# Seven-product output projection: blocks of positions change places, T2 and T3 are made within the attention, T1 and B11 are split where they are made

## The chip, the core and the metric

The kernel runs on one core of one Trainium2 chip. The engines named are PE (TensorE: matmuls and transposes), DVE (VectorE), ACT (ScalarE), POOL (GpSimd) and SP (SyncE), whose queue issues the transfers here. PEld is the weight load of PE. The metric is the device time of one execution in microseconds; before the change the median of three runs is 2041.89 us (2041.83 to 2044.91).

## What is computed

One layer of a hybrid decoder, in float32, on 2048 positions of width 1024:

```python
h = rmsnorm(x, norm1_g[l])
proj = h @ w_in[l]
p_q, p_k, p_v, p_g, p_a, c_b, c_c, c_h = jnp.split(proj, splits, axis=-1)
...
gate_logits = (p_a @ w_gate_up[l] + b_gate[l]).astype(jnp.float32)
log_a = (jax.nn.log_sigmoid(gate_logits) / GATE_NORMALIZER).reshape(bsz, seq, GLA_HEADS, GLA_DK)
o = gla_chunked(q, k, v, log_a)
o = rmsnorm(o, gla_norm_g[l]).astype(x.dtype)
o = o * jax.nn.silu(p_g.reshape(bsz, seq, GLA_HEADS, GLA_DV))
o_gla = o.reshape(bsz, seq, GLA_WIDTH)
u = c_c * c_h
o_conv = c_b * causal_depthwise_conv(u, conv_w[l])
mixed = jnp.concatenate([o_gla, o_conv], axis=-1) @ w_out[l]
x = x + mixed
h2 = rmsnorm(x, norm2_g[l])
ffn = (jax.nn.silu(h2 @ w_ffn_gate[l]) * (h2 @ w_ffn_up[l])) @ w_ffn_down[l]
x = x + ffn
```

A last RMSNorm follows. `gla_chunked` is causal gated linear attention with 4 heads (keys of 64, values of 128); the forget gate is low-rank. The short convolution has width 3 over 512 channels.

## The kernel before

**Products.** Each float32 operand is split into an upper part `hi` (rounded to a reduced float32 form, by ACT, L206) and a lower part `lo` (the rest, by DVE, L207). A product takes three matmuls, hi by hi, hi by lo and lo by hi (L503 to L505). A *unit* (`unit`) makes a 2 by 2 block product in seven block products instead of eight, in the manner of Strassen and Winograd: from the blocks B11, B12, B21, B22 of the moving side it needs T1 = B12 - B11, T2 = B22 - T1, T3 = B22 - B12 and T4 = T2 - B21 (up to sign), and from the weights S1 to S4. In each product four slices of 128 (`k`) are summed. Results go from PSUM by ACT as copies `c` (L549) or are added by DVE (L537).

**Positions and stages.** The 2048 positions form four blocks of 512; half 0 is blocks 0 and 1, half 1 is blocks 2 and 3. In time: the opening, the input projection of half 0 (to 269 us), that of half 1 (`in_proj(1)`, twelve units, 269 to 565), the output projection of half 0 by seven products (`out_proj_in_sevens`, four units, 565 to 666), that of half 1 by plain products (`out_proj`, from 666), then the FFN. For the seven products of the output projection the rows are the attention's output (`s_gla`) and the convolution's (`s_mix`), the columns blocks 0 and 1: B11 and B12 are the convolution's output of blocks 0 and 1, B21 and B22 the attention's.

**Order of the work.** PE runs the products. Beside them a list `background` holds generators (stepwise programs); `tick` is called after each block product and advances the first of them by one step at every second product, at every product while `hurry` is set, at three of four while `hasty` is set. At `in_proj(1)` the list holds a pause, `gate(1)` (the forget gate of half 1, hurried), `gla_half(0)` (the attention of half 0, eight chunks of 128 positions, hasty for its first 20 steps) and `mix_differences` (T3, T2 and T4, in four steps of 128 channels, hurried), then `gla_half(1)`, which runs on into the seven products. T1 is made and stored in `in_proj(0)`, in the conv units. `drain_background` runs what is left before the next stage starts. The scheduler places the instructions of a step on each engine's queue, and the engines work their queues in order. All transfers go through SP's queue, in order, a transfer waiting for one eight places back in a rotation.

**Operands.** The buffer `op` (28 of them, tag `op`) holds one block slice as a pair hi, lo. `load_pair` loads a stored pair; `load_undivided` loads a whole block, split later: at the end of the unit's second, fourth, fifth and sixth product for those named in `due`. In `mix_operands`, B11 and T1 are loaded whole and split before the first product; T2 is loaded as a pair; the rest are split by `due`. For half 1, `build_mix` loads pairs: the conv blocks of half 1 are split in `in_proj(1)` and stored as pairs, as are the attention's. `behind(marks)` orders an instruction behind given earlier ones, such as the last copy (`last_out`) or addition (`last_plus`).

## Time and profile before

| quantity | value |
|---|---|
| median of three runs | 2041.89 us |
| profiled execution | 2044.2 us |
| its span | 2042.4 us |
| PE busy | 2010.8 us, 98% |
| DVE busy | 77% |
| ACT busy | 48% |
| granted TensorE clock, mean | 0.993 |
| DMA, mean | 209 GB/s |

The page gives the span of one profiled execution, 1.8 us shorter than the execution's time. A row of the timeline reads: start, length, engine, line, operation, tile written <- tiles read, shape, count, and in brackets the idle time of that engine before it with what ended it. A row of the waits reads: engine, tile and line that waited <- what ended the wait, then us in total, times, longest. The shares of PE's chain go to the three product lines, 27 to 28% each.

### The profile page before, as it was taken

How to read it: one execution, taken by the hardware profiler on the slowest of the kernel's cores; microseconds unless marked ns; L12 is line 12 of the kernel's file. 1: busy time of each engine (PE TensorE's matmuls, PEld its weight loads, DVE VectorE, ACT ScalarE, POOL GpSimd, SP SyncE). 2: the span in 40 equal slices, each digit the busy share in tenths (PEclk: the TensorE clock that was granted, in tenths of full speed). 3: DMA queues.
4: the chain of work that ended last, by engine and by line, in shares of the span. 5: the costliest groups of instructions: out<-in, count | busy, mean ns of one | idle time of the engine just before them, and what ended most of it. 6: DMA issues, size and time to landing. Idle time of an engine off the chain costs nothing.

```text
span 2042.4 us, 27016 instructions
## 1 busy us (share of the span) xinstructions
PE 2010.8 (98%) x9251; PEld 1652.8 (81%) x9251; DVE 1574.5 (77%) x2831; ACT 981.9 (48%) x1941; POOL 10.3 (1%) x17
## 2 busy tenths in 40 slices
PE   9999999998989999999999999999999999999998
PEld 8888877787868888888888888887888888888886
DVE  7878868558887787778777688887777767778886
ACT  6664455654654344444444452334434444454345
POOL 0000000000000000000000000000000000000001
PEclk9999999999989999999999999999999999999998
DMA  7356865437687973446445576577444444486653
GB/s 263 128 202 219 285 260 176 135 122 266 194 277 246 346 269 134 170 171 219 164 159 196 192 292 242 188 283 292 157 168 170 158 147 170 175 331 221 247 216 129
DMA packets 192426, 427.78 MB, mean 209 GB/s; under 512 B 20544, under 2 KB 63776, under 8 KB 182816
## 3 DMA queue, kind: packets, MB, share of 16 engines
q1 hardware_dynamic: 191568, 425.40, 58.5%
q8 instruction: 73, 1.20, 0.2%
q10 hardware_dynamic: 720, 0.66, 0.1%
q14 instruction: 65, 0.53, 0.1%
HBM read 280.22 MB, written 145.75 MB: 209 GB/s over the span
## 4 chain that ended last, share of the span: by engine, by line
PE 94%; DVE 2%; ACT 2%; DMA 1%; issue 0%; SPq 0%; POOL 0%; POOLq 0%; DVEq 0%; ACTq 0%
PE mm L503 28%; PE mm L505 27%; PE mm L504 27%; PE mm L1394 1%; PE mm L1391 1%; PE mm L1392 1%; PE a_ps L1030 1%; PE mm L811 1%; PE mm L813 1%; PE mm L812 1%; PE o_ps L1211 1%; PE mm L1711 1%; DMA op<-sdT 1%; DVE wq L207 0%; PE o_ps L1218 0%
## 5 line engine op out<-in xcount | busy, mean ns | idle before, releaser
L503 PE MATMUL mm<-op,wq 128*128 128x512 f32 x2555 | 997.7, 393 | 9.2 <-ACT c L549 6.5
L504 PE MATMUL mm<-op,wq 128*128 128x512 f32 x2555 | 995.3, 390 | 0.0
L505 PE MATMUL mm<-op,wq 128*128 128x512 f32 x2555 | 985.9, 391 | 3.2 <-DVE wq L207 3.0
L206 ACT ACTIVATE wq<-raw 128x512 fp32r<-128x512 f32 (+2 forms) x620 | 362.1, 588 | 594.7 <-PE mm L505 500.3
L503 PEld LDWEIGHTS mm<-op,wq 128*128 128x128 f32 x2555 | 480.8, 188 | 115.9 <-ACT c L549 8.1
L505 PEld LDWEIGHTS mm<-op,wq 128*128 128x128 f32 x2555 | 480.7, 188 | 105.8 <-DVE wq L207 5.2
L504 PEld LDWEIGHTS mm<-op,wq 128*128 128x128 f32 x2555 | 481.1, 188 | 99.6 <-DVE op L207 1.5
L207 DVE TENSOR_TENSOR wq<-raw,wq 128x512 fp32r<-128x512 f32 (+2 forms) x620 | 390.9, 635 | 148.5 <-ACT wq L206 146.7
L537 DVE TENSOR_TENSOR y<-mm,y 128x512 f32<-128x512 f32 x213 | 145.6, 687 | 68.8 <-PE mm L505 67.9
L537 DVE TENSOR_TENSOR c<-mm,c 128x512 f32<-128x512 f32 x196 | 134.6, 687 | 74.3 <-PE mm L505 69.4
L549 ACT ACTIVATE c<-mm 128x512 f32<-128x512 f32 x198 | 115.3, 588 | 31.6 <-PE mm L505 28.4
L455 DVE TENSOR_TENSOR raw<-raw 128x512 f32<-128x512 f32 (+2 forms) x190 | 118.7, 631 | 2.2
L206 ACT ACTIVATE wq<-s 128x512 fp32r<-128x512 f32 (+2 forms) x100 | 58.9, 589 | 111.9 <-PE mm L505 98.5
L455 DVE TENSOR_TENSOR s<-raw 128x512 f32<-128x512 f32 (+2 forms) x95 | 60.0, 631 | 29.0 <-DMA raw<-in_wffn_dram 17.2
L207 DVE TENSOR_TENSOR op<-op 128x512 fp32r<-128x512 f32 x118 | 77.5, 682 | 3.7 <-ACT op L206 3.6
L206 ACT ACTIVATE op<-op 128x512 fp32r<-128x512 f32 x118 | 68.2, 621 | 11.4 <-DMA op<-sgla 5.2
L207 DVE TENSOR_TENSOR wq<-s,wq 128x512 fp32r<-128x512 f32 (+2 forms) x100 | 63.4, 634 | 2.1 <-ACT wq L206 1.3
L455 DVE TENSOR_TENSOR raw<-s,raw 128x512 f32<-128x512 f32 (+2 forms) x95 | 60.1, 633 | 1.4
L607 ACT ACTIVATE sg<-mm 128x512 f32<-128x512 f32 x26 | 15.5, 598 | 87.4 <-PE mm L505 87.3
L607 ACT ACTIVATE c<-c 128x512 f32<-128x512 f32 x78 | 48.9, 629 | 13.1 <-DVE c L537 10.5
L1392 PE MATMUL mm<-op,wq 128*128 128x512 f32 x128 | 50.2, 392 | 0.0
L1391 PE MATMUL mm<-op,wq 128*128 128x512 f32 x128 | 49.8, 389 | 0.0
(234 smaller groups left out, 1546.3 us busy)
## 6 DMA issues: line engine op xcount, KB each, us to landing
raw<-in_wffn_dram SPq DMA_DIRECT2D x44, 1024.0 KB, 6.2
sa_B<-so SPq DMA_DIRECT2D x47, 512.0 KB, 3.6
op<-sa_B SPq DMA_DIRECT2D x47, 512.0 KB, 6.5
raw<-in_win_dram SPq DMA_DIRECT2D x22, 1024.0 KB, 5.7
sa_T<-so SPq DMA_DIRECT2D x44, 512.0 KB, 4.4
op<-sa_T SPq DMA_DIRECT2D x44, 512.0 KB, 6.9
raw<-in_wdown_dram SPq DMA_DIRECT2D x24, 768.0 KB, 5.5
sx<-y SPq DMA_DIRECT2D x48, 256.0 KB, 4.1
```

Source lines behind the costliest of these rows:

```text
L206: last_hi[:] = [act.activation(hi, src, AF.Copy)]
L207: last_lo[:] = [dve.tensor_tensor(lo, src, hi.bitcast(F32), ALU.subtract)]
L455: dve.tensor_tensor(*args)
L503: pe.matmul(o[:], wh, xh, start=first and k == 0, stop=False, skip_group_check=True)
L504: pe.matmul(o[:], wh, xl, start=False, stop=False, skip_group_check=True)
L505: return pe.matmul(o[:], wl, xh, start=False, stop=k == n - 1, skip_group_check=True)
L537: last_plus[:] = [dve.tensor_tensor(t[:], o[:], t[:], ALU.add)]
L549: last_out[:] = [act.activation(t[:], o[:], AF.Copy)]
L607: last_silu[:] = [act.activation(s[:], c[:], AF.Silu)]
L811: pe.matmul(acc[:], wq[:, 0, c], p[:, 0, :], start=first, stop=False)
L1391: pe.matmul(o[e, j][:], wh, m[:, 0, :], start=n == 0, stop=False)
L1392: pe.matmul(o[e, j][:], wh, m[:, 1, :], start=False, stop=False)
```

## The change

The blocks change places: block 1's conv output becomes B11, block 0's B12, block 1's attention B21 and block 0's B22 (the residual `xt[1 - j]` and `s_x1[1 - j]` follow). T1 is then conv 0 - conv 1, T2 = attention 0 - T1 and T3 = attention 0 - conv 0, none of which needs block 1's attention; only T4 = T2 - attention 1 does.

- `gate(1)` is no longer hurried; it and what follows it run at three of four products (`hastened(..., 70)`).
- `mixes_early` makes T3 and T2 in four steps between the steps of the attention, once block 0's attention is done; T2 is split and stored as a pair and whole (`s_whole`). `mixes_late` makes T4 from the whole T2 after the attention. They use four small tiles (`mixed_tile`) instead of the tag of `h`.
- T1 and B11 are split in `in_proj(0)`, where they are made, and stored as pairs (`s_pair`), so `mix_operands` loads three operands as pairs.
- The conv blocks of half 1 are stored whole and split in `build_mix` (`load_whole`).
- In `in_proj(1)` the first two units, not three, have their weights prepared in step (`after=2`); `gla_half(1)` has one step more at its start.

```diff
@@ -113,11 +113,12 @@
-    s_mix = [
-        [dram.tile([P] + parts[b] + [PB], F32, name=f"sm{b}_{k}") for k in range(4)]
-        for b in range(NB)
-    ]
+    s_mix = scratch("sm", 4)
+    s_pair = {
+        n: [dram.tile([P, 2, PB], F32, name=f"sp{n}_{k}") for k in range(4)] for n in ("B11", "T1")
+    }
     s_gla = [dram.tile([P, HEADS] + parts[b] + [PB], F32, name=f"sgla{b}") for b in range(NB)]
+    s_whole = [dram.tile([P, PB], F32, name=f"sw{k}") for k in range(4)]
@@ -318,6 +319,7 @@
             if i == n:
                 hasty.clear()
             yield
+        hasty.clear()
 
     def h1_paced():
         with_marks.append(True)
@@ -1083,7 +1085,7 @@
             if half == 0:
                 yield unit(win[2], ops, raw=raw, between=between, rest=rest)
             for u in range(0 if half else 3, 12):
-                yield unit(win[u], ops, after=2 if half and u < 3 else None)
+                yield unit(win[u], ops, after=2 if half and u < 2 else None)
 
         units = units()
         for dst, i0 in ((s_kq, 0), (s_kq, 2), (s_v, 0), (s_v, 2)):
@@ -1119,19 +1121,20 @@
             for r, j, c, _ in next(units):
                 y = made[r, j] = cc[r, j]
                 dve.tensor_tensor(y[:], c[:], y[:], ALU.mult)
-                if half == 0:
-                    store(s_mix[j][i0 + r][:], y[:])
-                    if (r, 1 - j) in made:
-                        t1 = tt("t1")
-                        dve.tensor_tensor(t1[:], made[r, 1][:], made[r, 0][:], ALU.subtract)
-                        store(s_diff["T1"][i0 + r][:], t1[:])
-                    continue
-                hi = tp.tile([P, PB], F32R, name="hi", tag="t")
-                split(y[:], hi[:], y[:].bitcast(F32R))
-                dst = s_mix[2 * half + j][i0 + r]
-                store(dst[:, 0, :], hi[:].bitcast(F32))
-                store(dst[:, 1, :], y[:])
-
+                if half == 0 and (r, 1 - j) in made:
+                    t1 = tt("t1")
+                    dve.tensor_tensor(t1[:], made[r, 0][:], made[r, 1][:], ALU.subtract)
+                    store(s_diff["T1"][i0 + r][:], t1[:])
+                    store_pair(s_pair["T1"][i0 + r], t1)
+                    store_pair(s_pair["B11"][i0 + r], made[r, 1])
+                if half or j == 0:
+                    store(s_mix[2 * half + j][i0 + r][:], y[:])
+
+    def store_pair(dst, y):
+        hi = tp.tile([P, PB], F32R, name="hi", tag="t")
+        split(y[:], hi[:], y[:].bitcast(F32R))
+        for e, p in enumerate((hi[:].bitcast(F32), y[:])):
+            store(dst[:, e, :], p)
 
     def gla_half(half):
         chunks = [(b, t) for b in (2 * half, 2 * half + 1) for t in range(PT)]
@@ -1139,6 +1142,8 @@
             tables = act.preload_act_table_set("natural_log_exp_and_others")
         fetched = gla_fetch(*chunks[0])
         yield
+        if half:
+            yield
         with tc.issue_after(tables.ins):
             cur = gla_scaled(*fetched)
         yield
@@ -1150,6 +1155,7 @@
                 fetched = gla_fetch(*chunks[n + 1])
             if o is not None:
                 yield from gla_finish(*chunks[n - 1], *o)
+                done.add(chunks[n - 1])
             o = gla_outputs(b, t, *s)
             if n + 1 < len(chunks):
                 cur = gla_scaled(*fetched)
@@ -1287,57 +1293,66 @@
             act.activation(q[:], y, AF.Square)
             dve.tensor_tensor(ssq[:], ssq[:], q[:], ALU.add)
 
-    def mix_differences():
-        hurry.append(True)
-
-        def fetch(k):
-            tiles = []
-            for src in (s_mix[1][k][:], s_gla[1][:, k], s_diff["T1"][k][:], s_gla[0][:, k]):
-                tiles.append(bt("h"))
-                load(tiles[-1][:], src)
-            return tiles
-
-        def subtract(y, a, b):
-            with behind(last_plus):
-                dve.tensor_tensor(y[:], a[:], b[:], ALU.subtract)
-
-        tiles = fetch(0)
-        yield
+    def mixes_within(attention):
+
+        made = mixes_early()
+        for _ in attention:
+            yield
+            if (0, PT - 1) in done and next(made, True) is None:
+                yield
+        yield from made
+        yield from mixes_late()
+        done.add("mixes")
+
+    def mixed_tile(name, i):
+        tag = ("ssx0", "ssx1", "rb", "rb")[i]
+        return tiny.tile([P, PB], F32, name=name, tag=tag, bufs=1 if i < 2 else 2)
+
+    def mix_tiles(srcs, first=0):
+        tiles = [mixed_tile("mx", first + i) for i in range(len(srcs))]
+        for y, src in zip(tiles, srcs):
+            load(y[:], src)
+        return tiles
+
+    def subtract(y, a, b):
+        with behind(last_plus):
+            dve.tensor_tensor(y[:], a[:], b[:], ALU.subtract)
+
+    def mixes_early():
+
         for k in range(4):
-            b12, b22, t1, b21 = tiles
+            t1, b22, b12 = mix_tiles((s_diff["T1"][k][:], s_gla[0][:, k], s_mix[0][k][:]))
+            yield
             subtract(b12, b22, b12)
             store(s_diff["T3"][k][:], b12[:])
             subtract(b22, b22, t1)
-            if k < 3:
-                tiles = fetch(k + 1)
-            yield
-            subtract(b21, b21, b22)
-            store(s_diff["T4"][k][:], b21[:])
-            hi = bx[0].tile([P, PB], F32R, name="hi", tag="b")
+            store(s_whole[k][:], b22[:])
+            hi, lo = mixed_tile("hi", 3), t1
             with behind(last_out + last_plus):
-                split(b22[:], hi[:], b22[:].bitcast(F32R))
-            for e, p in enumerate((hi, b22)):
-                store(s_diff["T2"][k][:, e, :], p[:].bitcast(F32))
-            yield
-        hurry.clear()
-        done.add("mixes")
-
-    def hurried(steps):
-        hurry.append(True)
-        yield from steps
-        hurry.clear()
+                split(b22[:], hi[:].bitcast(F32R), lo[:].bitcast(F32R))
+            for e, y in enumerate((hi, lo)):
+                store(s_diff["T2"][k][:, e, :], y[:])
+            yield
+
+    def mixes_late():
+        for k in (0, 2):
+            pairs = [
+                mix_tiles((s_whole[k + i][:], s_gla[1][:, k + i]), 2 * i) for i in range(2)
+            ]
+            yield
+            for i, (t2, b21) in enumerate(pairs):
+                subtract(t2, b21, t2)
+                store(s_diff["T4"][k + i][:], t2[:])
+            yield
 
     def mix_operands():
-        src = {"B11": [y[:] for y in s_mix[0]], "B21": [s_gla[0][:, k] for k in range(4)]}
-        src.update({"B22": [s_gla[1][:, k] for k in range(4)], **s_diff})
+        src = {"B21": [s_gla[1][:, k] for k in range(4)]}
+        src.update({"B22": [s_gla[0][:, k] for k in range(4)], **s_diff, **s_pair})
         ops = no_operands()
         for _, n in PRODUCTS:
-            ops[n] = [(load_pair if n == "T2" else load_undivided)(p) for p in src[n]]
-            if n in ("B11", "T1"):
-                with behind(last_out):
-                    for o in ops[n]:
-                        split(o[:, 1, :].bitcast(F32), o[:, 0, :], o[:, 1, :])
-            elif n != "T2":
+            paired = n in ("B11", "T1", "T2")
+            ops[n] = [(load_pair if paired else load_undivided)(p) for p in src[n]]
+            if not paired:
                 undivided[n] = ops[n]
         return ops
 
@@ -1348,7 +1363,7 @@
                 y[r, j] = tt("y")
             else:
                 y[r, j] = tiny.tile([P, PB], F32, name="y", tag="rb")
-            load(y[r, j][:], xt[j, :, d0 + r, :])
+            load(y[r, j][:], xt[1 - j, :, d0 + r, :])
         return y
 
     def out_proj_in_sevens(first, ops):
@@ -1368,13 +1383,16 @@
             unit(None, ops, onto=onto[d0], raw=quads, midway=more)
             for r, j in ((0, 0), (1, 1), (0, 1), (1, 0)):
                 y = onto[d0][r, j]
-                store(s_x1[j][d0 + r][:], y[:])
-                sum_squares(ssq[j], y[:], d0 == 0 and r == j)
+                store(s_x1[1 - j][d0 + r][:], y[:])
+                sum_squares(ssq[1 - j], y[:], d0 == 0 and r == j)
         return ssq
 
     def build_mix():
         def pair(b, k):
-            return load_pair(s_gla[b][:, k] if k < HEADS else s_mix[b][k - HEADS])
+            if k < HEADS:
+                return load_pair(s_gla[b][:, k])
+            with behind([all_plus[-4]] if k < HEADS + 2 else last_out + last_plus):
+                return load_whole(s_mix[b][k - HEADS])
 
         return {k: [pair(2 + j, k) for j in range(2)] for k in LATE_HEADS}
 
@@ -1800,7 +1818,7 @@
     drain_background()
     ops = load_pairs(s_h1)
     background.extend(
-        [pause(3), hurried(gate(1, ops)), hastened(gla_half(0), 20), mix_differences()]
+        [pause(3), hastened(chain(gate(1, ops), mixes_within(gla_half(0))), 70)]
     )
     in_proj(1, ops)
     drain_background(lambda: "mixes" in done)
```

`load_whole`, not shown in the diff, is `load_undivided` followed by a split.

The counts of matmuls, DVE and ACT instructions are the same in both orders; SP has twelve transfers more. Three places follow in which rows stand differently. Line numbers in the new order are one to eighteen higher.

ACT, in a conv unit of `in_proj(1)`, where PE waits for a copy `c` at 493 us. Before (`h` and `hi` are the mixes' tiles and the conv splits, `ee` the attention's decays):

```order
L206 ACTIVATE hi<-h 128x512
L206 ACTIVATE wq<-raw 128x512
L206 ACTIVATE hi<-c_4505 128x512
L1173 ACTIVATE ee<-ee 128x256
L1174 ACTIVATE ee<-ee 128x256
L206 ACTIVATE hi<-c_4519 128x512
L206 ACTIVATE hi<-c_4618 128x512
L549 ACTIVATE c_5059<-mm 128x512
L549 ACTIVATE c_5094<-mm 128x512
```

The same unit in the changed kernel, up to the copy of the same place (`c_5076`):

```order
L551 ACTIVATE c_4952<-mm 128x512
L1207 ACTIVATE carry<-state_110,em 128x128
L1179 ACTIVATE ee<-ee 128x256
L1180 ACTIVATE ee<-ee 128x256
L207 ACTIVATE wq<-raw 128x512
L207 ACTIVATE wq<-s_5027 128x512
L207 ACTIVATE wq<-raw 128x512 x2
L551 ACTIVATE c_5076<-mm 128x512
```

The splits `hi<-h` and `hi<-c` no longer stand ahead of the copies.

ACT, in the first unit of the seven products, up to the copies of `kt_ps` and `v_ps` (PSUM tiles of the attention, the chunk that PE waits for near 580 us). Before:

```order
L206 ACTIVATE op<-op 128x512
L206 ACTIVATE hi<-c_5168 128x512
L206 ACTIVATE wq<-raw 128x512
L206 ACTIVATE op<-op 128x512 x3
L212 ACTIVATE hl<-hsq 128x4
L206 ACTIVATE op<-op 128x512
L1201 ACTIVATE carry<-state_109,em 128x128
L213 ACTIVATE hy<-hl 128x4
L206 ACTIVATE hi<-c_5312 128x512
L1196 ACTIVATE ee<-kt_ps 128x256
L1197 ACTIVATE vt<-v_ps 128x512
```

The changed kernel, a chunk of attention at the same place:

```order
L207 ACTIVATE op<-op 128x512
L213 ACTIVATE hl<-hsq 128x4
L214 ACTIVATE hy<-hl 128x4
L207 ACTIVATE op<-op 128x512
L207 ACTIVATE wq<-raw 128x512
L1207 ACTIVATE carry<-state_109,em 128x128
L207 ACTIVATE op<-op 128x512
L207 ACTIVATE wq<-raw 128x512
L207 ACTIVATE op<-op 128x512 x2
L1202 ACTIVATE ee<-kt_ps 128x256
L207 ACTIVATE op<-op 128x512 x2
L1203 ACTIVATE vt<-v_ps 128x512
```

From the `vt` copy of one chunk to the `ee` copy of the next, thirteen `op` splits and four `hi` splits stood on ACT before; now eight `op` splits stand there, and the conv splits `hi<-c` are gone. The eight `op` splits of B11 and T1, ahead of this place before, are gone too.

PE, at the change from the seven products to the plain output projection (L1391 before, L1409 after, is its first product line). Before, the last transposes `ot` of the attention stand among the seven products' matmuls:

```order
L505 MATMUL mm<-op,wq 128x512
L1261 MATMUL ot<-ident,osb 128x128 x3
L503 MATMUL mm<-op,wq 128x512
L504 MATMUL mm<-op,wq 128x512
L505 MATMUL mm<-op,wq 128x512
```

The changed kernel:

```order
L1409 MATMUL mm<-op,wq 128x512
L1410 MATMUL mm<-op,wq 128x512
L1409 MATMUL mm<-op,wq 128x512
L1267 MATMUL ot<-ident,osb 128x128 x3
L1410 MATMUL mm<-op,wq 128x512
L1412 MATMUL mm<-op,wq 128x512 x2
```

They now stand behind the output projection's first matmuls.

More of the change, by code (lines that the diff above doesn't have):

```diff
@@ L1310, in mix_differences @@
             subtract(b22, b22, t1)
-            if k < 3:
-                tiles = fetch(k + 1)
-            yield
-            subtract(b21, b21, b22)
-            store(s_diff["T4"][k][:], b21[:])
-            hi = bx[0].tile([P, PB], F32R, name="hi", tag="b")
-            with behind(last_out + last_plus):
-                split(b22[:], hi[:], b22[:].bitcast(F32R))
-            for e, p in enumerate((hi, b22)):
-                store(s_diff["T2"][k][:, e, :], p[:].bitcast(F32))
-            yield
-        hurry.clear()
-        done.add("mixes")
-    def hurried(steps):
-        hurry.append(True)
-        yield from steps
-        hurry.clear()
+            store(s_whole[k][:], b22[:])
+            hi, lo = mixed_tile("hi", 3), t1
+            with behind(last_out + last_plus):
+                split(b22[:], hi[:].bitcast(F32R), lo[:].bitcast(F32R))
+            for e, y in enumerate((hi, lo)):
+                store(s_diff["T2"][k][:, e, :], y[:])
+            yield
+    def mixes_late():
[3 more added lines that the diff above has]
+            ]
+            yield
+            for i, (t2, b21) in enumerate(pairs):
+                subtract(t2, b21, t2)
+                store(s_diff["T4"][k + i][:], t2[:])
+            yield
     def mix_operands():
-        src = {"B11": [y[:] for y in s_mix[0]], "B21": [s_gla[0][:, k] for k in range(4)]}
-        src.update({"B22": [s_gla[1][:, k] for k in range(4)], **s_diff})
+        src = {"B21": [s_gla[1][:, k] for k in range(4)]}
+        src.update({"B22": [s_gla[0][:, k] for k in range(4)], **s_diff, **s_pair})
         ops = no_operands()
         for _, n in PRODUCTS:
-            ops[n] = [(load_pair if n == "T2" else load_undivided)(p) for p in src[n]]
-            if n in ("B11", "T1"):
-                with behind(last_out):
-                    for o in ops[n]:
-                        split(o[:, 1, :].bitcast(F32), o[:, 0, :], o[:, 1, :])
-            elif n != "T2":
+            paired = n in ("B11", "T1", "T2")
+            ops[n] = [(load_pair if paired else load_undivided)(p) for p in src[n]]
+            if not paired:
                 undivided[n] = ops[n]
```

## The prediction

> **What bounds the kernel now.** I read the page's busy shares and chain first, then the waits of PE, then stretches of the span, then single instructions.
>
> ```profile
> span 2042.4 us, 27016 instructions
> PE 2010.8 (98%) x9251; PEld 1652.8 (81%) x9251; DVE 1574.5 (77%) x2831; ACT 981.9 (48%) x1941; POOL 10.3 (1%) x17
> ```
>
> PE is busy for 2010.8 of 2042.4 us, so 31.6 us of idle time is all that moving work can win back, beside matmuls that run slowly. The change adds no matmul and removes none. So the question is where PE idles, and whether the change reaches those places. It touches the input projection of the second half and the seven products after it, from 260 to 680 us. PE's waits from 260 to 760 us (engine, line, waited for, then us in total, times, longest):
>
> ```profile
> PE mm L503 <- ACT c L549: 5.4, 2, 4.9
> PE v_ps L1195 <- ACT ee L1196: 4.2, 1, 4.2
> PE kt_ps L1192 <- DVE c L1121: 3.1, 1, 3.1
> PE mm L505 <- DVE wq L207: 3.0, 2, 2.6
> PE mm L503 <- ACT op L206: 1.0, 1, 1.0
> PE mm L503 <- DVE y L537: 0.9, 1, 0.9
> ```
>
> That is 17.6 us, over half of PE's idle time, in eight waits. The timeline places them, and shows the matmuls behind them:
>
> ```profile
> 271.30 1.02 PE L503 MATMUL mm<-op,wq 128*128 128x512 f32 x2 [1.04 <-ACT op L206]
> 317.74 0.50 PE L505 MATMUL mm<-op,wq 128*128 128x512 f32 x1 [2.57 <-DVE wq L207]
> 321.02 0.63 PE L505 MATMUL mm<-op,wq 128*128 128x512 f32 x1
> 493.21 0.80 PE L503 MATMUL mm<-op,wq 128*128 128x512 f32 x1 [4.86 <-ACT c L549]
> 497.18 0.40 PE L505 MATMUL mm<-op,wq 128*128 128x512 f32 x1
> 577.70 0.44 PE L1192 MATMUL kt_ps<-ident,kq 128*128 128x128 f32 x2 [3.15 <-DVE c L1121]
> 582.30 1.11 PE L1195 MATMUL v_ps<-ident,vt 128*128 128x128 f32 x4 [4.17 <-ACT ee L1196]
> 583.07 0.78 PE L503 MATMUL mm<-op,wq 128*128 128x512 f32 x1
> 588.31 0.39 PE L503 MATMUL mm<-op,wq 128*128 128x512 f32 x1
> 588.54 0.39 PE L504 MATMUL mm<-op,wq 128*128 128x512 f32 x1
> ```
>
> After a long wait the matmuls also start further apart. The last two rows stand 0.23 us apart, the usual spacing. From 583.07 to 588.31 there are twelve starts in 5.24 us; at 0.23 us they take 2.76, so 2.5 us are lost. From 493.21 to 497.18 there are eleven in 3.97, so 1.4 are lost; from 317.74 to 321.02 nine in 3.28, so 1.2. Three places thus cost:
>
> - near 317 us: 2.57 + 1.2 = 3.8;
> - from 460 to 500 us: 0.4 (the second of the two 3.0 us of `wq` waits) + 0.5 (the second of the two of `c`) + 4.86 + 1.4 = 7.2;
> - at the start of the seven products: 3.15 + 4.17 + 0.9 + 2.5 = 10.7.
>
> Together 21.7 us. What causes them is seen in stretches (start:end, length, then busy us of PE, PEld, DVE, ACT, POOL, the granted clock, the DMA share and GB/s):
>
> ```profile
> 210.00:215.00 5.00, 5.00 (x22) 3.89 (x22) 5.00 (x10) 3.31 (x6) 0.00 (x0) 1.00 0.75 279
> 270.00:275.00 5.00, 3.94 (x17) 2.79 (x16) 4.71 (x8) 5.00 (x11) 0.00 (x0) 1.00 1.05 404
> 315.00:320.00 5.00, 2.43 (x9) 1.84 (x8) 5.00 (x14) 1.17 (x4) 0.00 (x0) 0.86 0.62 180
> 440.00:460.00 20.00, 20.00 (x91) 16.45 (x91) 10.60 (x24) 8.77 (x24) 0.00 (x0) 1.00 0.39 117
> 460.00:480.00 20.00, 19.10 (x83) 15.16 (x82) 20.00 (x33) 9.91 (x18) 0.00 (x0) 1.00 0.73 259
> 480.00:500.00 20.00, 15.14 (x68) 11.93 (x67) 17.42 (x31) 8.46 (x16) 0.00 (x0) 0.91 0.91 308
> 575.00:580.00 5.00, 0.44 (x2) 0.20 (x2) 5.00 (x11) 5.00 (x11) 0.00 (x0) 0.80 1.06 392
> 580.00:585.00 5.00, 2.69 (x9) 2.31 (x10) 5.00 (x12) 3.76 (x10) 0.00 (x0) 0.50 1.02 396
> 660.00:680.00 20.00, 20.00 (x90) 16.57 (x89) 8.60 (x14) 5.37 (x9) 0.00 (x0) 1.00 1.03 410
> ```
>
> In all three DVE is busy without a break: 5.00 of 5 at 315, 20.00 of 20 at 460, 5.00 of 5 at 575 and 580. Just beside them it has room: 10.60 of 20 at 440, 8.60 of 20 at 660. So these are local crowds on DVE (and on ACT at 575), which spreading can cure.
>
> [...]
>
> **The change, part by part.** *The gate at 3 of 4 steps.* Before, the four gates of the second half run at every product, and their scans (sixteen L1072, four L1069, three L1076 between 305 and 320 us) crowd DVE; the weight's lower half `wq` comes 2.57 us late. Spread by a third, the weight split moves ahead of the crowd. I count on all but 0.3 of the 3.8; the bounds are 0 (the crowd only shifts) and 3.8. Gain 3.5.
>
> *T2 and T3 within the attention; the four conv blocks of this half no longer split here.* DVE's groups between 460 and 500 us (count, busy us, mean ns):
>
> ```profile
> L1302 DVE TENSOR_TENSOR h<-h 128x512 f32<-128x512 f32 x12 | 8.1, 685 | 1.8 <-DMA h<-sgla 1.8
> L207 DVE TENSOR_TENSOR c<-c,hi 128x512 fp32r<-128x512 f32 x4 | 2.7, 688 | 0.0
> L207 DVE TENSOR_TENSOR h<-h,hi 128x512 fp32r<-128x512 f32 x4 | 2.7, 686 | 0.0
> ```
>
> Twenty instructions, 13.5 us, of DVE's 37.4 in these 40 us. After the change only the four subtractions for T4 stay near here, 2.7 us; the other twelve mix operations (8.2 us) move to a stretch with 9.4 of 20 us free, and the conv splits to the end of the seven products. The 4.86 us wait had ACT in it too: its splits of `h` and `c` stood before the copy `c` L549 that PE waited for, behind loads of `ee` that queued behind stores on SP. Neither kind stands there afterwards. Gain 6.2 of 7.2; bounds 0 and 7.2.
>
> The mix loads now follow stores on SP's in-order queue, and the subtractions wait in order on DVE:
>
> ```profile
> 460.61 6.46 SPq L163 DMA_DIRECT2D sdT<-h  x3
> ```
>
> Here three dependent stores occupied 6.46 us of the queue. The same now happens within the attention, where behind it stand loads of `raw` weights, of `kq`, `ee`, `vt`. With DVE half free I take 0 as its cost to PE, with 6.5 (one such hold in the open) as the bound. [...]
>
> *T1 and B11 split where they are made.* This removes eight splits from the run-up to the seven products, and of half 1's eight conv splits the four late ones leave its first products. At the wait near 577 us:
>
> ```profile
> L207 DVE TENSOR_TENSOR op<-op 128x512 fp32r<-128x512 f32 x15 | 9.9, 680 | 1.1 <-ACT op L206 1.1
> L207 DVE TENSOR_TENSOR c<-c,hi 128x512 fp32r<-128x512 f32 x3 | 2.0, 681 | 0.0
> L206 ACT ACTIVATE op<-op 128x512 fp32r<-128x512 f32 x15 | 9.0, 624 | 2.2 <-DMA op<-sgla 1.8 <-DMA op<-sdT 0.4
> ```
>
> Those fifteen `op` splits between 570 and 590 belong to the next four operands and remain (sixteen in all), with the DMA at a share of 1.06. What leaves is the three `c` splits, 2.0 us each on DVE and ACT, and the eight before. And where ACT worked through thirteen `op` and four `hi` splits between one chunk's copy of `v_ps` and the next chunk's copy of `kt_ps`, eight `op` splits now stand; the nine that leave are 9 x 0.62 = 5.6 us of ACT, against the 7.3 us that `kt_ps` and `v_ps` waited. I expect 2.7 of 10.7 to stay. Gain 8; bounds 0 (the same loads at a full DMA hold the same chain) and 10.7.
>
> The eight splits are done earlier instead. Four fall near 210 us, where DVE is busy 5.00 of 5: 4 x 0.69 = 2.7 us at most, 0 if weights are far enough ahead; one load of weights already waited 0.30 there:
>
> ```profile
> 213.27 0.19 PEld L505 LDWEIGHTS mm<-op,wq 128*128 128x128 f32 x1 [0.30 <-DVE wq L207]
> ```
>
> I take 1.0. The other four, with six more stores of 256 KB net, fall near 270 us, where the DMA moves 404 GB/s at a share of 1.05: 1.57 MB take 3.9 us. The operand loads of the next unit queue with them, and PE already waits 1.04 at 271.30. Between 0 and 3.9 I take 1.2, two stores ahead of those loads.
>
> *The eight splits of half 1's conv blocks* now stand at the end of the seven products and after. Cover: DVE has 11.4 and ACT 14.6 of 20 us free at 660; loads of 512 KB become 256. Cost 0; without the cover, 8 x 0.69 = 5.5.
>
> *The attention of the second half* begins a step later and at fewer products. In the new order its last transposes `ot` stand after the output projection's first matmuls, where before they stood well ahead:
>
> ```profile
> 649.88 0.49 PE L1261 MATMUL ot<-ident,osb 128*128 128x128 f32 x3
> 654.83 0.52 SPq L163 DMA_DIRECT2D sgla<-osb  x1
> 657.63 5.66 SPq L160 DMA_DIRECT2D op<-sgla  x6
> op<-sgla SPq DMA_DIRECT2D x8, 512.0 KB, 8.7
> ```
>
> Before: 4.95 us from `ot` to the store of its block, 2.8 to the first loads, 8.7 until one lands (the last row, of the view of DMA issues from 650 to 675 us): 16.5 us. Between the last `ot` and the first matmul that uses that block the new order has 50 matmuls: 11.5 us. So the wait is at most 5.0; it is 0 if the chain runs tighter, since DVE has more room there and the loads of the conv blocks halve. I take 2.0, nearer the lower end.
>
> **Sum.** Gains 3.5 + 6.2 + 8.0 = 17.7, costs 1.0 + 1.2 + 2.0 = 4.2: net 13.5. The profiled execution took 2044.2 us, 1.8 of it outside the span, and stands 2.3 over the median of 2041.9; its waits are taken to be the median's. 2041.9 - 13.5 = **2028 us**. All gains and no cost would give 2041.9 - 21.7 = 2020.
>
> **Rivals.** *The transition keeps its wait*: sixteen `op` splits remain of those at 570 to 590, and the DMA share of 1.06 means their loads come no sooner. Against it, nine splits leave ACT's queue ahead of the awaited copy. Gain 8 lost: 2036.
>
> *Everything is hidden*, as the free DVE time at 440 and 660 allows: 2020.
>
> *Slower: the mixes hold SP's queue.* Six steps (four early, two late) each have stores that wait for DVE, and loads behind them that wait for stores. If each holds the queue for 6.46 us, and that outruns the lead of the weights, PE stops each time and then runs slowly for 1.4 more: 7.9 a step. It makes the kernel slower from three steps in the open (3 x 7.9 + 4.2 > 17.7 + 4.1), and four give 2041.9 + 31.6 + 4.2 - 17.7 = 2060. For it: the hold was there at 460, with PE waiting behind it. Against it: then DVE was full, and now it is half free.
>
> *The change does not do what it says*: the crowd just moves, DVE's work being the same; gains halve to 8.9 and costs rise to their bounds, 2.7 + 3.9 + 5.0 = 11.6: 2045, about no change.
>
> **How the numbers follow.** The forecast 0.52 (its own range 2022 to 2034), the transition kept 0.18, all hidden 0.08, no net change 0.08, slower 0.14. A measurement can tell 0.2% from no change, 4.1 us. Faster: 0.52 + 0.18 + 0.08 = 0.78, with the no-change case mostly in same: 0.07, and slower 0.15. The range runs from 2018 to 2045: it leaves out the slower case and little else.
>
> **What would show it.** Right: no wait over 1 us near 317 and 490, DVE below 18 of 20 in every 20 us of 460 to 500, busier than 10.60 in 440 to 460; at the start of the seven products under 3 us of idle and a granted clock over 0.8; a wait under 4 us at the output projection's first use of the last attention block. Wrong: waits of PE for `wq` or `raw` between 380 and 480 with SP standing in stores; the transition's waits still at 7 us or more; over 4 us lost near 210 or 270.

## The result, and the profile after

The changed kernel takes 2057.78 us (median of 4 runs, 2055.63 to 2060.46) where the kernel before takes 2042.99 (4 runs, 2041.83 to 2044.91): a ratio of 1.0072, 95% interval 1.0055 to 1.0090. The change makes it slower by 15 us; 2028 was forecast, and 2018 to 2045 was the range. The profiled execution is the slowest of the four, 2060.46 us, with a span of 2058.8. From the page after, the span, the busy time of each engine, and the chain of work that ended last, by engine:

```profile
span 2058.8 us, 27018 instructions
PE 2016.6 (98%) x9251; PEld 1654.8 (80%) x9251; DVE 1573.3 (76%) x2831; ACT 981.1 (48%) x1941; POOL 10.3 (0%) x17
PE 89%; DMA 5%; DVE 3%; SPq 1%; ACT 1%; issue 1%; POOL 0%; POOLq 0%; ACTq 0%; DVEq 0%
```

The work is the same, as the counts of instructions show. PE idles 42.2 us (2058.8 - 2016.6) where it idled 31.6, and the chain, which gave 94% to PE and 1% to transfers before, now gives 89% and 5%. PE's waits from 180 to 760 us:

```profile
PE mm L505 <- ACT c L551: 13.1, 4, 8.3
PE mm L505 <- ACT op L207: 6.8, 2, 5.1
PE mm L505 <- DVE c L539: 2.8, 2, 1.9
PE ot L1267 <- DVE osb L1258: 2.8, 2, 1.9
PE mm L505 <- ACT wq L207: 1.8, 1, 1.8
```

The names before are gone: nothing waits for `kt_ps`, `v_ps`, or a weight's lower half. In their place stand 13.1 us for ACT's copies of results. PE's timeline of the changed kernel has them here:

```profile
213.09 0.50 PE L505 MATMUL mm<-op,wq 128*128 128x512 f32 x1 [3.17 <-ACT c L551]
228.92 0.50 PE L505 MATMUL mm<-op,wq 128*128 128x512 f32 x1 [1.89 <-DVE c L539]
281.04 0.79 PE L505 MATMUL mm<-op,wq 128*128 128x512 f32 x1 [8.26 <-ACT c L551]
288.25 0.51 PE L505 MATMUL mm<-op,wq 128*128 128x512 f32 x1 [1.72 <-ACT op L207]
549.92 0.50 PE L505 MATMUL mm<-op,wq 128*128 128x512 f32 x1 [1.21 <-ACT c L551]
554.85 0.30 PE L1267 MATMUL ot<-ident,osb 128*128 128x128 f32 x1 [1.91 <-DVE osb L1258]
589.58 0.77 PE L505 MATMUL mm<-op,wq 128*128 128x512 f32 x1 [5.08 <-ACT op L207]
611.16 0.50 PE L505 MATMUL mm<-op,wq 128*128 128x512 f32 x1 [1.79 <-ACT wq L207]
681.64 0.30 PE L1267 MATMUL ot<-ident,osb 128*128 128x128 f32 x1 [0.85 <-DVE osb L1258]
```

Stretches of the changed kernel, columns as before:

```profile
200.00:220.00 20.00, 16.83 (x74) 13.59 (x73) 19.08 (x32) 9.11 (x16) 0.00 (x0) 1.00 0.78 255
260.00:280.00 20.00, 12.78 (x57) 10.25 (x55) 10.10 (x16) 4.20 (x7) 0.00 (x0) 0.91 1.03 400
280.00:300.00 20.00, 16.93 (x54) 12.75 (x55) 14.47 (x24) 10.63 (x20) 0.00 (x0) 0.75 0.61 228
460.00:480.00 20.00, 20.00 (x108) 15.96 (x108) 16.23 (x32) 9.15 (x28) 0.00 (x0) 1.00 0.48 164
480.00:500.00 20.00, 20.00 (x94) 16.35 (x93) 17.23 (x34) 9.90 (x20) 0.00 (x0) 1.00 0.54 161
580.00:600.00 20.00, 14.39 (x68) 11.30 (x66) 16.39 (x37) 13.45 (x33) 0.00 (x0) 0.83 0.95 324
```

From 460 to 500 us the crowd is gone: PE is busy 20.00 of 20 and DVE 16 to 17. The new hole is at the change of halves. Between 260 and 280 us PE is busy 12.78 of 20 while DVE has half and ACT four fifths of its time free; they wait too, with the DMA at a share of 1.03.

To compare kernels, the loss of a stage is counted in one way for all: PE's idle time by the brackets of its timeline, plus 0.2 us for each start of a product's matmul 0.38 to 0.46 us after the matmul ahead, where 0.23 is usual (a row of several matmuls is taken apart into its starts). Stages are bounded by the number of the matmul, so that they mean the same work in every kernel. In us, idle and slow starts together:

| stage (time in the kernel before) | before | after |
|---|---|---|
| end of half 0's projection (200 to 235) | 0.0 | 5.1 |
| start of half 1's (265 to 295) | 1.0 | 13.9 |
| gates (near 317) | 3.8 | 0.4 |
| conv units and mixes (460 to 500) | 6.8 | 0.0 |
| last conv units (500 to 565) | 0.0 | 4.1 |
| seven products (565 to 650) | 10.4 | 8.8 |
| change to the plain products | 0.0 | 0.9 |
| whole kernel, to its last product | 25.3 | 37.5 |

The count explains 12.2 of the 16.4 us between the two spans; the rest lies in smaller gaps and in attention matmuls that start slowly, which it leaves out.

**How the 8.26 us come about.** The timeline of the changed kernel, rows of SP's queue, ACT and DVE in order of time:

```profile
269.25 4.06 SPq L161 DMA_DIRECT2D op<-siB  x3
269.52 0.63 ACT L207 ACTIVATE hi<-t 128x512 fp32r<-128x512 f32 x1 [2.04 <-DVE t L1126]
273.67 0.32 SPq L164 DMA_DIRECT2D sdT<-t  x1
274.28 0.63 ACT L207 ACTIVATE hi<-c 128x512 fp32r<-128x512 f32 x1 [4.12 <-DMA sm<-c]
274.95 0.32 SPq L164 DMA_DIRECT2D spT<-hi  x1
279.00 0.69 DVE L208 TENSOR_TENSOR t<-t,hi 128x512 fp32r<-128x512 f32 x1 [3.36 <-DMA sdT<-t]
280.39 0.60 ACT L551 ACTIVATE c<-mm 128x512 f32<-128x512 f32 x1 [5.48 <-DMA spT<-hi]
```

ACT copies the first product of the new unit out of PSUM at 280.39, after 5.48 us of idle time that a *store* ended: that of T1's `hi`, issued at 274.95. The copy needs one of the nine tiles of the pool `tp`, tag `t`, into which results go; `store_pair` took `hi` from that pool, and it came free only when its store had landed, 5.4 us later, with the DMA at a share of 1.03. ACT had written that `hi` at 269.52 already: its store first stood 4.8 us in SP's queue, behind loads of `op` and the store of the whole T1. So the tile was held for 10.9 us (269.52 to 280.39), almost half of it before its store began. The split ahead of it (`hi<-c`) had waited 4.12 us for a store in the same way, and DVE's `t<-t,hi`, which writes T1's lower part over T1, for the store of the whole T1. So three engines stood while 256 KB stores went through: PE for 8.26 us, ACT for 4.12 and 5.48, DVE for 3.36.

### The profile page after: what moved, and what is told of

The parts are those of the page before. It is cut to its first block, busy times and chain, and to the rows that moved or that the text cites. A ratio compares the mean times of both kernels' runs of the same rounds, so it can differ in the third digit from the quotient of the medians.

```text
span 2058.8 us, 27018 instructions
## 1 busy us (share of the span) xinstructions
PE 2016.6 (98%) x9251; PEld 1654.8 (80%) x9251; DVE 1573.3 (76%) x2831; ACT 981.1 (48%) x1941; POOL 10.3 (0%) x17
## 4 chain that ended last, share of the span: by engine, by line
PE 89%; DMA 5%; DVE 3%; SPq 1%; ACT 1%; issue 1%; POOL 0%; POOLq 0%; ACTq 0%; DVEq 0%
PE mm L505 26%; PE mm L506 26%; PE mm L507 26%; PE mm L1412 1%; PE mm L1409 1%; PE mm L1410 1%; SPq L161 1%; DMA op<-shT 1%; PE mm L813 1%; PE a_ps L1032 1%; PE mm L815 1%; PE mm L814 1%; PE mm L1729 1%; DMA raw<-in_win_dram 1%; DMA raw<-in_wout_dram 1%
## 5 line engine op out<-in xcount | busy, mean ns | idle before, releaser
L609 ACT ACTIVATE c<-c 128x512 f32<-128x512 f32 x78 | 48.8, 629 | 13.1 <-DVE c L539 10.5
L1409 PE MATMUL mm<-op,wq 128*128 128x512 f32 x128 | 48.9, 390 | 0.0
```

The costliest lines, as they stand in the source:

```text
L609: last_silu[:] = [act.activation(s[:], c[:], AF.Silu)]
L1409: pe.matmul(o[e, j][:], wh, m[:, 0, :], start=n == 0, stop=False)
```

## The experiments

The first five undo the pair stores, keep the pairs or only `hi` in other tiles, put the pair stores alone into the kernel before, and undo the gate's pace. The ratio is always to the kernel before, run beside it on the same chip.

**T1 and B11 not paired.**

```diff
-                    store_pair(s_pair["T1"][i0 + r], t1)
-                    store_pair(s_pair["B11"][i0 + r], made[r, 1])
-                if half or j == 0:
+                if half < 2:
                     store(s_mix[2 * half + j][i0 + r][:], y[:])
...
-            paired = n in ("B11", "T1", "T2")
+            paired = n == "T2"
             ops[n] = [(load_pair if paired else load_undivided)(p) for p in src[n]]
-            if not paired:
+            if n in ("B11", "T1"):
+                with behind(last_out):
+                    for o in ops[n]:
+                        split(o[:, 1, :].bitcast(F32), o[:, 0, :], o[:, 1, :])
+            elif not paired:
                 undivided[n] = ops[n]
```

> The change with T1 and B11 stored whole and split at the start of the seven products, as before; all else as in the change. Theory: the pair stores made in the conv units cost the waits at 213 and 229 us (3.2 + 1.9) and at 281 to 289 us (8.3 + 1.7 + 0.3 of idle and some 4.5 of slow matmuls), 20 us of the changed kernel. Without them these are gone but for about 1 us, the eight splits cost up to 3 us where the seven products start: 2040 us (2037 to 2045). Rival, the loss comes from the gate's pace or the mixes within the attention: 2056 or more, with the waits near 281 still there.

Measured: 2042.55 us (10 runs), ratio to before 1.0003 (0.9991 to 1.0015). The waits near 213 and 229 are gone and 1.0 is left near 271, as expected: 18.0 us of the table. But the seven products lose 11.8 us, nearly all in a single wait:

```profile
565.90 0.45 PE L1265 MATMUL ot<-ident,osb 128*128 128x128 f32 x1 [11.60 <-DVE osb L1256]
```

**The same pairs, in small tiles.** The stores and their bytes stay; `hi` and `lo` go to the four tiles that the mixes use later.

```diff
     def store_pair(dst, y):
-        hi = tp.tile([P, PB], F32R, name="hi", tag="t")
-        split(y[:], hi[:], y[:].bitcast(F32R))
-        for e, p in enumerate((hi[:].bitcast(F32), y[:])):
+        hi, lo = [mixed_tile("pr", 2 * (dst in s_pair["B11"]) + e) for e in range(2)]
+        split(y[:], hi[:].bitcast(F32R), lo[:].bitcast(F32R))
+        for e, p in enumerate((hi[:], lo[:])):
```

> The change with its pair stores, the same bytes in the same order, but hi and lo of T1 and B11 in four small tiles outside the pool of nine that results are copied into, and lo not written over T1 or B11. Theory one, held tiles: ACT's copy of a result waits because hi sits in that pool until its store is through, and lo waits for the store of the whole T1 that it overwrites; then the wait at 281 falls under 3 us and the time is near 2043 us. Theory two, bytes: six more stores at a full DMA push the operand loads back, whatever tile they come from; then PE still idles over 6 us between 270 and 295 and the time stays at 2054 or more.

Measured: 2043.21 us (10 runs), ratio 0.9998 (0.9987 to 1.0009). Its stretch at the change of halves:

```profile
260.00:280.00 20.00, 19.96 (x88) 16.00 (x87) 13.40 (x22) 11.17 (x20) 0.00 (x0) 1.00 1.05 407
280.00:300.00 20.00, 20.00 (x89) 16.43 (x88) 13.27 (x22) 14.28 (x26) 0.00 (x0) 1.00 0.59 213
```

The DMA is as full as in the changed kernel (1.05, 407 GB/s) and PE idles 0.04 us instead of 7.2. The bytes cost PE nothing there, and the kernel's time falls by 14.6 us with the other tiles.

**Only `hi` in a small tile**, `lo` still written over T1 and B11.

> The change with only hi of the pairs in small tiles; lo is still written over T1 and B11 in the pool of results, after the store of the whole T1 that reads the same tile. If the tile held by hi is what ACT's copy waits for, PE's wait of 8.3 us near 281 falls under 3. If the write of lo over T1, and T1 and B11 staying in the pool until lo is stored, is what counts, over 5 us stay.

Measured: 2044.85 us (one run), and near 281 this is all that is left:

```profile
271.44 1.02 PE L505 MATMUL mm<-op,wq 128*128 128x512 f32 x2 [0.37 <-ACT op L207]
```

So it is the tile held by `hi`. The write over T1 is as in the change, and PE is busy 19.61 of 20 us from 260 to 280 and 20.00 from 280 to 300, where the change has 12.78 and 16.93.

**The pair stores alone, in the kernel before** (its `store_pair` as in the change, T1 and B11 loaded as pairs):

> The kernel before with this one part of the change: T1 and B11 split in the conv units and stored as pairs, the blocks in their old places. If the pair stores alone cost what the change lost, waits of 10 us or more appear between 265 and 295 us and some near 213, and up to 3 us are won at the start of the seven products: 2058 us. Rival, they cost only with the new order of blocks: 2040 us.

Measured: 2064.3 us (4 runs), ratio 1.0101 (1.0086 to 1.0117). The waits come with that part alone, 3.5 near 213 and 13.0 at the change of halves, while the other waits of before stay (4.4 near 317, 7.7 in the conv units):

```profile
278.29 0.79 PE L506 MATMUL mm<-op,wq 128*128 128x512 f32 x1 [7.01 <-ACT c L552]
334.44 0.60 PE L508 MATMUL mm<-op,wq 128*128 128x512 f32 x1 [2.60 <-DVE wq L210]
```

Here the seven products lose 5.5 us instead of 10.4: the early splits do help them, in the old arrangement.

**The gate hurried, in the change** (`hurried(gate(1, ops))` ahead of the rest in the list again):

> The change with the gate of half 1 at every product again. If the gate's slower pace is what removed the wait of 2.6 us for a weight near 317 us, that wait comes back: +3.5, 2061 us. Rival: the slower pace makes the attention late, which is why it still crowds the seven products; then the waits of 5.1, 1.8 and 0.9 us at 590, 611 and 682 us shrink, and the time is 2053 us.

Measured: 2062.53 us (4 runs), ratio 1.0100 (1.0083 to 1.0117). Slower than the change by 4.8 us, but not as either line says: there is no wait near 317 us. The loss is later:

```profile
518.58 0.80 PE L505 MATMUL mm<-op,wq 128*128 128x512 f32 x1 [3.00 <-DVE c L539]
612.54 0.80 PE L505 MATMUL mm<-op,wq 128*128 128x512 f32 x1 [6.67 <-ACT wq L207]
```

That left the question what removed the wait near 317, and two kernels answer it.

**Two units prepared in step, not three, in the kernel before:**

```diff
-                yield unit(win[u], ops, after=2 if half and u < 3 else None)
+                yield unit(win[u], ops, after=2 if half and u < 2 else None)
```

> The kernel before with one detail of the change: only two units, not three, have their weights prepared in step. With the gate hurried in the changed kernel the wait of 2.6 us near 317 did not come back, so the pace is not what removed it. Theory: the third unit's weights, prepared in step behind additions, were the late ones; then that wait goes here, with its slow matmuls: 2039 us. Rival: it went because products moved against the gates (mixes and pace); then it stays, 2043 us.

Measured: 2040.57 us (10 runs), ratio 0.9983 (0.9974 to 0.9993). The loss near 317 is 0.0, with the gate's crowd in its place. The first row is the kernel before, the others are this one:

```profile
317.02 1.87 DVE L207 TENSOR_TENSOR wq<-raw,wq 128x512 fp32r<-128x512 f32 x3
310.00:315.00 5.00, 5.00 (x23) 4.14 (x23) 5.00 (x13) 2.61 (x6) 0.00 (x0) 1.00 0.62 206
315.00:320.00 5.00, 5.00 (x30) 3.66 (x30) 5.00 (x14) 2.92 (x8) 0.00 (x0) 1.00 0.54 156
```

DVE is busy 5.00 of 5 as before, and PE now is too. Before, three splits of the third unit's weights stood together behind the gate's scans, and PE's wait at 317.74 ended with the first of them. Here such splits stand among the scans, at 308.73, 309.94, 313.28 and 315.24 us.

**Only the gate's pace, in the kernel before:**

```diff
-        [pause(3), hurried(gate(1, ops)), hastened(gla_half(0), 20), mix_differences()]
+        [pause(3), hastened(gate(1, ops), 70), hastened(gla_half(0), 20), mix_differences()]
```

> The kernel before with the gate of half 1 at three of four products instead of every one, and nothing else. The prediction put the end of the wait near 317 us down to this pace. If the pace is enough, the 3.8 us near 317 go, 2040 us; if the third unit's weights prepared in step are the cause, a wait for wq over 1 us stays between 300 and 330, 2043 us.

Measured: 2041.26 us (10 runs), ratio 0.9985 (0.9975 to 0.9994). The wait is thinned out, not gone: 2.1 us are lost near 317 instead of 3.8, of which the weights' part (`wq`) is 1.0.

```profile
314.88 0.72 PE L1186 MATMUL sc<-kq 64*128 64x128 f32 x8 [1.14 <-DVE kq L1176]
318.10 0.50 PE L505 MATMUL mm<-op,wq 128*128 128x512 f32 x1 [0.78 <-DVE wq L207]
```

**Why the seven products gain so little.** With the tiles mended the change still only equals the kernel before. Three kernels look at its loss there, which is 11.8 us with the pairs in small tiles, and 3.1 in the last conv units. The expectations of the first two count those conv units with the seven products: their 14.9 is 11.8 + 3.1.

*Half 1's attention earlier* (no extra step at its start, `hastened(gla_half(half), 60)` instead of 12, pairs in small tiles):

> The change with its pairs in small tiles, and the attention of half 1 begun without the extra step and advanced at three of four products all the way instead of for twelve steps. In the change PE still loses 12.7 us (idle and slow matmuls) in the seven products, against 10.4 before, and 14.7 where T1 and B11 are not paired. Theory, late attention: more chunks of half 1's attention now fall into the seven products, whose operand splits stand ahead of its instructions on DVE and ACT; then the loss there falls under 8 us and the time is 2037 us. Rival, the operand loads and splits themselves hold PE whenever the attention comes: the loss stays at 11 or more, 2043 us.

Measured: 2042.28 us (10 runs), ratio 0.9995 (0.9985 to 1.0005). The rival: 14.5 us are lost in the seven products, among others in these waits:

```profile
565.90 0.33 PE L1265 MATMUL ot<-ident,osb 128*128 128x128 f32 x1 [2.66 <-DVE osb L1256]
595.40 0.79 PE L505 MATMUL mm<-op,wq 128*128 128x512 f32 x1 [4.50 <-ACT wq L207]
```

*The next unit's weights asked for earlier* (pairs in small tiles):

```diff
-        onto = {0: first}
+        onto, raws = {0: first}, {0: raw_weights(wout[0])}
 
         def fetch(d0):
+            raws[d0] = raw_weights(wout[d0 // 2])
             onto[d0] = residual(d0)
...
```

> The change with its pairs in small tiles and the next unit's weights asked for earlier in the same way. Without it PE lost 14.9 us in the seven products, 4.1 of idle in a wait for weights at 592 us. Theory, SP's order: that wait goes with the slow matmuls behind it, 2043 - 5 = 2038 us, the other waits of that stage (9 us) stay. Rival: the stage as a whole is bound by DVE's and ACT's splits and the full DMA, and the loss stays near 14 us: 2043.

Measured: 2041.72 us (10 runs), ratio 0.9988 (0.9976 to 1.0000). PE's wait for weights is gone, others have grown, and the loss is 11.4 where it was 11.8, as the rival has it. The longest now:

```profile
570.15 0.50 PE L505 MATMUL mm<-op,wq 128*128 128x512 f32 x1 [3.48 <-ACT op L207]
600.91 0.30 PE L1267 MATMUL ot<-ident,osb 128*128 128x128 f32 x1 [3.46 <-DVE osb L1258]
```

*Both together:*

> The change with three repairs together: pairs in small tiles, half 1's attention begun without the extra step and at three of four products throughout, and the next unit's weights asked for earlier. On SP's queue the loads of two chunks of attention (28 transfers) stand between the operand loads of the seven products in the change; with the attention's earlier phase it is one chunk, as before, and the weights come ahead of the next. Theory, the order on SP's queue decides the loss in the seven products: 14.5 us there fall to 7 or less, as in the kernel before with three parts (6.0), 2035 us. Rival: the stage is bound by splits on DVE and ACT, and another wait takes the place: loss 12 or more, 2041 us.

Measured: 2039.57 us (10 runs), ratio 0.9984 (0.9974 to 0.9993). No wait of PE for `op` or for weights is left in that stage; the loss is 10.8 us all the same, and its longest waits now bear DVE's name:

```profile
565.17 0.47 PE L1265 MATMUL ot<-ident,osb 128*128 128x128 f32 x1 [2.83 <-DVE osb L1256]
598.98 1.22 PE L1190 MATMUL sc<-kq 64*128 64x128 f32 x8 [3.35 <-DVE kq L1180]
```

Neither line is met: the loss did not fall to 7, and the splits are not shown to be the limit. Shortly ahead of both waits ACT or DVE itself stood idle for a load (4.12 and 2.95 us), and the attention's instructions came behind it, DVE's last `kq` at 598.51:

```profile
562.12 0.63 ACT L207 ACTIVATE op<-op 128x512 fp32r<-128x512 f32 x1 [4.12 <-DMA op<-sgla]
595.50 0.69 DVE L457 TENSOR_TENSOR s<-raw 128x512 f32<-128x512 f32 x1 [2.95 <-DMA raw<-in_wout_dram]
```

So loads still stand behind these two waits, 6.2 of the 10.8 us, one step further back: on the engines that feed PE.

**Parts of the change in the old arrangement.** First the pairs in small tiles alone:

> The kernel before, blocks and mixes as there, with T1 and B11 split early into small tiles and stored as pairs. With the pairs in the pool of results the seven products lost 5.5 instead of 10.4 us, but 12.6 came in between 265 and 295 and 3.5 near 213. If held tiles were all of that cost, it is gone and the gain stays: 2038 us. If the order of the blocks before also matters (T3 made from block 1, its loads next in the queue), some 5 us of waits stay near 280: 2043 us.

Measured: 2044.32 us (10 runs), ratio 1.0004 (0.9995 to 1.0014). The cost at the change of halves is gone (1.5 us left), but the conv units lose 8.1 and the seven products 8.3: the gain of 4.9 seen above shrinks to 2.1. The time is the second line's, but not for its reason, since 1.5 and not 5 us are lost near 280. (The 12.6 of the expectation is 13.0 in the table below.)

Then pairs in small tiles, two units in step, and half 1's conv blocks split in `build_mix` as in the change:

> The kernel before with three parts of the change and not the others: T1 and B11 as pairs by small tiles, two units prepared in step, and the conv blocks of half 1 split in the output projection's loads. The blocks keep their places and the mixes stay after the attention. Sum of the losses of before: 3.8 near 317 (gone), 6.8 between 460 and 500 (two thirds gone, since four conv splits of its twenty instructions leave, and those that stood ahead of the awaited copy), 10.4 in the seven products (5.5 left): 2043 - 3.8 - 4.5 - 4.9 = 2030 us. Rival: the late conv splits take DVE time that the seven products need, 5 us: 2035; and if the parts only trade places, 2043.

Measured: 2039.10 us (10 runs), ratio 0.9978 (0.9968 to 0.9987), short of the sum and of the first rival. The loss near 317 is 0.0 and that of the conv units 1.9. The seven products lose 7.4, nearly all in one wait, for weights whose load SP's queue issues from 586.35 us, behind the attention's load of `gt` at 585.87:

```profile
591.57 0.63 ACT L206 ACTIVATE wq<-raw 128x512 fp32r<-128x512 f32 x1 [3.13 <-DMA raw<-in_wout_dram]
592.25 0.79 PE L503 MATMUL mm<-op,wq 128*128 128x512 f32 x1 [6.79 <-ACT wq L206]
```

Last the same with the next unit's weights asked for earlier:

> The kernel before with three parts of the change, and the output projection's weights for the next unit asked for at the middle of the unit, ahead of its residual rows and so ahead of a chunk of attention on SP's queue: 18 transfers earlier. Without this the three parts left one wait of 6.8 us in the seven products, for weights whose load lands 5 us after it is issued, behind the attention's fourteen loads. Theory, SP's order: the wait goes, 2039 - 6 = 2033 us. Rival, the splits on a full DVE or the DMA itself hold PE there: the wait only changes its name, 2038 us or more.

Measured: **2036.94 us** (7 runs, 2033.12 to 2040.02), ratio 0.9965 (0.9953 to 0.9976): 0.35% faster than the kernel before. PE's wait for weights is gone. What comes next in that stage is short:

```profile
593.28 0.72 PE L1195 MATMUL sc<-kq 64*128 64x128 f32 x8 [1.78 <-DVE kq L1185]
```

Of the 6.8 us that wait had cost the stage got back only 1.4 (7.4 to 6.0), and the two intervals overlap: that the weights' order makes this kernel faster than the one ahead is not shown.

Loss by stage, in us as in the table above, for the kernels that carry the reading:

| stage | before | change | not paired | small tiles | three repairs | before + pairs | before + three parts, weights first |
|---|---|---|---|---|---|---|---|
| 200 to 235 | 0.0 | 5.1 | 0.0 | 0.2 | 0.2 | 3.5 | 0.5 |
| 265 to 295 | 1.0 | 13.9 | 1.0 | 0.2 | 0.2 | 13.0 | 1.5 |
| near 317 | 3.8 | 0.4 | 0.0 | 0.2 | 0.2 | 4.4 | 0.0 |
| 460 to 500 | 6.8 | 0.0 | 0.0 | 0.0 | 0.0 | 7.7 | 2.7 |
| 500 to 565 | 0.0 | 4.1 | 3.1 | 3.1 | 4.8 | 0.0 | 0.8 |
| seven products | 10.4 | 8.8 | 11.8 | 11.8 | 10.8 | 5.5 | 6.0 |

## Why the prediction was wrong, point by point

*What bounds the kernel.* Right: the losses lay in the three crowds, and those the change reached did move.

*T1 and B11 split where they are made: the step that failed.* The prediction took 1.0 us near 210 us, as DVE time, and 1.2 near 270, as bytes in a full DMA. The stages lose 5.1 and 12.9 more than before. Its upper bounds, 2.7 and 3.9, are both passed, because it priced engines and bytes only. The term it left out is the tile: `hi` in a pool of nine, held until a store lands, and ACT's copy of the next result behind it. The two kernels with `hi` elsewhere show it, with the same stores at a DMA share of 1.05 (1.03 in the change). This term alone makes the kernel slower: 2057.8 with it, 2043.2 without, against 2043.0 before. It does not account for the gain that failed to come.

The trace of the changed kernel shows how long a store can hold its tile: the one issued at 274.95 released ACT 5.4 us later, at 280.39. The prediction looked for a hold by stores at the mixes alone, on SP's queue (6.46 us), where little came of it, and not in the tiles that the pairs' stores held.

*T2 and T3 within the attention, conv splits moved.* Right: 6.2 us were counted, and the loss of 6.8 went to 0.0. The hold on SP's queue that made the slower rival cost PE at most 1.4 us between 325 and 460, all of PE's idle time there (busy 133.56 of 135.00). But 3 us of waits or more appeared in the last conv units in all kernels of the changed arrangement, of which the prediction has nothing; their cause stays open.

*The gate's pace.* The size is right (3.5 counted, 3.4 gained) and the cause is wrong. Preparing two units in step, a detail that the prediction gave no term, removes the wait with the gate as hurried as before; the pace alone takes 1.7 of the 3.8. That the size came out is luck.

*The transition.* Wrong: a gain of 8 was counted, 1.6 came. The splits that left had not been the limit alone. When one wait was taken away there, others were left or grew: for operands (3.48 us) and `osb` (3.46) once the weights came earlier, for `kq` (3.35) with all three repairs, there behind 2.95 us in which DVE itself stood for a load. This is the first rival's outcome (the transition keeps its wait), though its reason, the loads of the remaining sixteen operands, explains part of it only. Why the old arrangement with the same pairs loses 5.5 to 8.3 us there and the arrangement of the change 8.8 to 14.5 is not settled: the attention's phase and SP's order were tried and do not decide it by themselves.

*The end of the attention.* Right in place, smaller: 2.0 us counted, 0.9 measured.

*The slower case* had the right sign and the wrong place. Not the mixes' stores but the pairs' stores were it, a hundred microseconds and more ahead. That its 2060 lies near the measured 2057.8 is luck. One of the prediction's signs of being wrong did come: over 4 us lost near 210 and near 270.

*The sum.* By the table the gains are 3.4 + 6.8 + 1.6 = 11.8, where 17.7 were counted, and the costs 5.1 + 12.9 + 4.1 + 0.9 = 23.0, where 4.2 were.

## What to carry to other kernels

When work is moved earlier, count the buffers it holds until its stores land as a cost of its own, beside engine time and bytes (here a tile was held for 10.9 us, and the kernel was 14.6 us faster with other tiles); ask which instruction needs the next buffer of that pool, and what stands behind it. Give a store's staging tile a pool that no result copy draws from. Do not count the longest wait of a stage as the gain from taking it away: in the seven products one of 6.8 us went and 1.4 came back. And a wait that bears an engine's name is to be followed back: that engine may have stood for a load just before, as ACT did here for 4.12 us and DVE for 2.95.

## What the runs showed that was not expected

With the DMA at a share of 1.05 from 260 to 280 us PE idled 0.04 us when the pairs stood in small tiles; with the same stores and a share of 1.03 it idled 7.2 in that stretch when their `hi` was taken from the nine tiles that results need. And a DVE busy 5.00 of 5 from 305 to 320 us cost PE 3.8 us in the kernel before and 0.0 with two units in step, by the place of three weight splits among its instructions.
